# Down projection: accumulators first written by ScalarE, the residual added in later blocks, stores in SP's queue

## The chip, the cores and the metric

The kernel runs on one core of one Trainium2 chip. A core has a matrix engine (TensorE, PE in the profile, with PEld for its weight loads), VectorE (DVE), ScalarE (ACT), GpSimd (POOL) and SyncE (SP), which run their own instruction streams and meet through semaphores. Matmuls write to PSUM, a small memory of banks of 128 x 512 fp32; DVE and ACT read it, POOL does not here. DMA transfers are issued by SP, ACT or POOL, each from its own in-order queue, and run beside the engines. The metric is the device time of one execution in microseconds; the median of three runs is compared.

## The reference

One inference step of one hybrid encoder layer, for a prompt of 1024 frames and a running stream of 64 frames, together 1088 rows of width 1024:

```python
h = _rms_norm(x, norm1_g)
parts = jnp.split(h @ w_in, np.cumsum(IN_SIZES)[:-1].tolist(), axis=-1)
...
x = x + jnp.concatenate([o_a, o_b, o_c], axis=-1) @ w_out
h = _rms_norm(x, norm2_g)
x = x + (jax.nn.silu(h @ w_gate) * (h @ w_up)) @ w_down
```

The three mixers between the two projections (a gated delta rule, a gated MLP over chunks, a sliding-window attention) do not matter here. What matters is the first norm of `x`, at the very start, and the last line: its hidden layer has 2816 columns, `w_down` is 2816 x 1024, and `x` on the right is the residual.

## The kernel before

**Number format.** Every fp32 operand of a matmul is kept as two numbers, a rounded one (`h`, made by an ACT copy) and the remainder (`l`, a DVE subtraction); a product takes three matmuls, hh, hl and lh.

**The start.** `x_load` (L254) brings a tile of 128 rows of `x`; its third argument is the issuing queue, POOL by default. SP issues x tile 0, then three weight loads with x tile 2 and the constants behind them; x tile 1 goes through POOL's queue (L270). `x_stat` (L290) sums squares on ACT (L293) and forms the reciprocal root on POOL with `gpow` (L284: a multiply-add, L287, and a power, L288). L315 does this for tiles 0 and 1, L316 and L317 scale both tiles on DVE, and everything that follows is released after the second scaling (`issue_after(first.ins)`). Then PE transposes the tiles (L303), DVE applies the gain, ACT rounds, and the input projection's matmuls (L95) run against weights split by `Weights.split` (L133: ACT copy into `hw`, DVE subtraction into `lw`).

**The down projection** (L1652 to L1958) runs over six blocks of hidden columns, `KB`: five of two groups of 256, the last of one. In a block there are four pairs of prompt tiles (`PAIRS`), each with seven steps (`STEPS`, a Strassen-like scheme in which step results are added along the way inside a PSUM bank), and two sample steps for the 64 stream rows. A step of a prompt pair has 6 matmuls of 128 x 512 (3 in block 5), a sample step 8 (4 in block 5), all from L1803 and L95. Block 0 runs pair 0, the sample, then pairs 1 to 3; the others begin with the sample.

After every step its bank is added to an accumulator `yf[t]`, a 128 x 1024 tile in SBUF. `y_add` (L1778) does that on DVE, reading PSUM and `yf`, writing `yf`. The step after next in the same bank (banks Y and Z; X is used once) accumulates onto what is there, so PE waits for the addition. In the sample the lower 64 partitions of the bank are first copied by ACT, and DVE makes two additions. The accumulator starts as the residual: `y_load` (L1772) takes a place in SBUF and loads the tile from `yd` in SP's queue, two tiles before block 0 and seven in it, at the steps in `y_when` (L1931).

In block 5 the additions of steps 0, 1 and 2 go through an ACT copy and a POOL addition (L1816, L1817). Those of steps 3 to 6 are the last of their halves: DVE adds, and `y_out` (L1782) stores 128 x 512 from ACT's queue. The two stream halves are stored after the first step of pair 1 (`outs`).

**Loads.** The hidden operand of a step, `w<-hd`, is loaded by `a_load` (L1759) into one of 20 slots of the pool `WS`. `fetch` (L1866) issues one load a step while the dictionary `AL` holds fewer than nine entries (seven while hidden stores are left). A step takes its entry out of `AL` (L1798); a sample step reads its entry and leaves it there (L1831). The weights `w_down` are loaded (L1698), combined on POOL (`diff`, L1706), rounded on ACT (`rnd`) and split on DVE (`sub`) for the next block at the step numbers in `ORDER`, through `prep` (L1750). In block 0 the last hidden values are also still being split and stored from ACT's queue by `hidden_late` (L1553).

**Order.** From the last unit of the hidden layer on, `manual_schedule` keeps all engines, SP among them, in the program's order: for each step the matmuls, the step's addition with its store if it has one (`flush`), `fetch`, residual loads, hidden stores, sample stores, `prep` (L1933 to L1952).

Of the kernel before, what the change touches and what calls it, by code (L numbers as in the profile page):

```python
# [12 lines left out]
ALU = mybir.AluOpType  # L13
# [40 lines left out]
def hybrid_step(ctx, tc, x_prompt, x_sample, cache_k, cache_v, st_gdn, st_conv, norm1_g, w_in, conv_w, a_log,  # L54
# [3 lines left out]
    V, A, G, T, SP = nc.vector, nc.scalar, nc.gpsimd, nc.tensor, nc.sync  # L58
# [17 lines left out]
    def sb(p, shape, tag, dt=F32, bufs=None):  # L76
        return p.tile(shape, dt, tag=tag, name=tag, bufs=bufs)
# [7 lines left out]
    def acopy(out, in_, scale=1.0):  # L85
        return A.activation(out=out, in_=in_, func=AF.Copy, scale=scale)  # L86
# [4 lines left out]
    def tt(out, in0, in1, op):  # L91
        return V.tensor_tensor(out=out, in0=in0, in1=in1, op=op)  # L92
# [155 lines left out]
    def x_rows(s, t):  # L248
        t0, np_, ns = SEGS[s]
        return (x_prompt[0, t0 + 128 * t:t0 + 128 * t + 128, :], 128) if 128 * t < np_ else (x_sample[0], 64)  # L250

    xs_tiles = {}

    def x_load(s, t, q=G):  # L254
        src, r = x_rows(s, t)
        x = sb(xp, [128, DM], "xs", bufs=3)
        q.dma_start(out=x[:r], in_=src)
        xs_tiles[s, t] = x
# [7 lines left out]
    prm1 = sb(gp, [128, 390], "tr", bufs=9)  # L266
    A.dma_start(out=prm1[0:8, 0:128], in_=norm1_g[0].rearrange("(k p) -> k p", p=128))
    W.load()
    W.load()
    x_load(0, 1)  # L270
    W.load()
    x_load(0, 2, SP)
    SP.dma_start(out=cst[:, 192:], in_=cst_in[:, 192:])
# [16 lines left out]
    def x_stat(x, r):  # L290
        jk = sb(wp, [128, DM], "xt2", BF16, bufs=2)
        ss = sb(cp, [128, 1], "ss", bufs=4)
        A.activation(out=jk[:r], in_=x[:r], func=AF.Square, accum_out=ss[:r])  # L293
        gpow(ss[:r], ss[:r], 1.0 / DM, EPS, mhalf)
        return ss
# [16 lines left out]
            acopy(h, t[:, :, :r])  # L312
            tt(xl[:, 4 * j:4 * j + 4, c0:c0 + r], t[:, :, :r], h.bitcast(F32), ALU.subtract)

    rstd = [x_stat(xs_tiles[0, t], 128) for t in range(2)]  # L315
    for t in range(2):  # L316
        first = V.tensor_scalar(out=xs_tiles[0, t], in0=xs_tiles[0, t], scalar1=rstd[t], scalar2=None, op0=ALU.mult)  # L317
    pb = ax()
    T.transpose(pb[:, :8], prm1[0:8, 0:128], ident[0:8, 0:8])
    g1T = sb(cp, [128, 8], "g1T")  # L320
    V.tensor_copy(out=g1T, in_=pb[:, :8])
    ctx.enter_context(tc.issue_after(first.ins))
    W.run(1)
    prm = sb(gp, [128, 390], "tr", bufs=9)
    SP.dma_start(out=prm[0:8, 0:128], in_=norm2_g[0].rearrange("(k p) -> k p", p=128))
    SP.dma_start(out=prm[8:9, 0:128], in_=gdn_g)
# [888 lines left out]
    yd = tc.dram_tile([9 * 128, DM], F32, name="yd")  # L1215
# [201 lines left out]
    WS = Slots([128, 4, 128])  # L1417
# [236 lines left out]
    PAIRS = ((0, 0, 0, 2), (0, 1, 1, 3), (1, 0, 4, 6), (1, 1, 5, 7))  # L1654
    RIGHT = ("B11", "T1", "T2", "B21", "T3", "B22", "T4")
    LAST = {0: "R1", 4: "T13", 5: "R2", 6: "T24"}
    D, AL, yf = {}, {}, {}
# [20 lines left out]
    y_places, outs = [], []  # L1678

    def block(t):  # L1680
        return t.rearrange("p a b -> p (a b)")
# [87 lines left out]
        SP.dma_start(out=v[:, :2 * len(kps)].bitcast(F32),  # L1769
                     in_=hs[2 * kps[0]:2 * kps[-1] + 2].rearrange("f p t -> p f t"))  # L1770

    def y_load(t, places=y_places):  # L1772
        p, tag, bufs = places.pop(0)
        yf[t] = sb(p, [128, DM], tag, bufs=bufs)
        r = 64 if t == 8 else 128
        SP.dma_start(out=yf[t][:r], in_=yd[128 * t:128 * t + r, :])

    def y_add(t, h, ps):  # L1778
        c = slice(512 * h, 512 * h + 512)
        tt(yf[t][:, c], ps, yf[t][:, c], ALU.add)  # L1780

    def y_out(t, h):  # L1782
        c = slice(512 * h, 512 * h + 512)
        dst = y_p[0, 128 * t:128 * t + 128, c] if t < 8 else y_s[0, :, c]
        A.dma_start(out=dst, in_=yf[t][:dst.shape[0], c])


    STEPS = ((0, "Y", ((0, 0, 0),)), (1, "Z", ((1, 1, 0),)), (2, "Y", ((0, 1, 0),)), (3, "X", ((0, 0, 1),)),
# [2 lines left out]
    def pair_steps(b, p):  # L1791
        kps, banks = KB[b], {}

        def step(n, bank, adds):
            fresh = bank not in banks
            if fresh:
                banks[bank] = mmb() if bank == "X" else ax()
            ps, a = banks[bank], AL.pop((b, p, n))  # L1798
            m = 0
            for k, kp in enumerate(kps):  # L1800
                bh, bl = D[kp][RIGHT[n]]
                for l, r in ((a[:, 2 * k], bh), (a[:, 2 * k], bl), (a[:, 2 * k + 1], bh)):
                    T.matmul(ps, l, r, start=fresh and m == 0, stop=m == 3 * len(kps) - 1,  # L1803
                             skip_group_check=not fresh)
                    m += 1
                if p == 3 and n in LAST:
                    PT.give(D[kp][LAST[n], "h"], D[kp][LAST[n], "l"])
            WS.give(a)

            def add():  # L1810
                for i, j, done in adds:
                    t = PAIRS[p][2 + i]
                    if b + 1 == len(KB) and not done:
                        slot = WS.take()
                        c = slice(512 * j, 512 * j + 512)
                        acopy(block(slot), ps)  # L1816
                        G.tensor_tensor(out=yf[t][:, c], in0=block(slot), in1=yf[t][:, c], op=ALU.add)  # L1817
                        WS.give(slot)
                        continue
                    y_add(t, j, ps)  # L1820
                    if done and b + 1 == len(KB):
                        y_out(t, j)
            later.append(add)

        return [lambda x=x: step(*x) for x in STEPS]

    def sample_steps(b):
        kps = KB[b]

        def step(j):  # L1830
            ps, v = ax(), AL[b]  # L1831
            m, last = 0, 4 * len(kps) - 1
            for k, kp in enumerate(kps):
                for i in range(2):
                    for w in D[kp]["B%d%d" % (i + 1, j + 1)]:
                        mm(ps, v[:, 2 * k + i], w, m == 0, m == last)
                        m += 1
            if j:
                WS.give(v)

            def add():
                slot = WS.take()
                tmp = block(slot)[:64]
                c = slice(512 * j, 512 * j + 512)
                acopy(tmp, ps[64:128, :])
                tt(yf[8][:64, c], ps[0:64, :], yf[8][:64, c], ALU.add)
                tt(yf[8][:64, c], tmp, yf[8][:64, c], ALU.add)
                WS.give(slot)
                if b + 1 == len(KB):
                    outs.append(lambda: y_out(8, j))  # L1850
            later.append(add)

        return [lambda j=j: step(j) for j in range(2)]
# [32 lines left out]
    for u in range(22):  # L1886
        if u == 21:
            ctx.enter_context(tc.manual_schedule(engines=ENGINES))
        sa, sb_ = unit_steps(u, 0), unit_steps(u, 1)
        if u == 0:  # L1890
            sa = [lambda: None] * 3 + [begun[k] for k in (2, 4, 5, 6)]
        steps = sa + sb_ if u in (0, 21) else [s for p in zip(sa, sb_) for s in p]
        for i, s in enumerate(steps):
            s()
            flush()
            for q in hid[:1] if u < 21 else ():
                if next(q, 1):
                    hid.remove(q)
            if u == 0 and i < 7:
                next(xs1, None)  # L1900
            if i >= 7 or u not in (0, 21):
                n = i - 7 if u in (0, 21) else i // 2
                if u in (0, 21) or i % 2:
                    WS.give(*WA[u].pop(PRODUCTS[n][0]))
            if i == 7 - (u > 0) and u + 1 < 22:
                w_sums(u + 1)
            if i >= 7 and u + 1 < 22:
                for n in ([i - 8] if 7 < i else []) + ([6] if i == 13 else []) if u == 0 else [i - 7]:
                    w_split(u + 1, PRODUCTS[n][0])
            if u == 21:  # L1910
                left_over(i)
                prep(0, i)
                if i in (7, 8):
                    y_load(PAIRS[0][i - 5])
                if i > 7:
                    fetch()
            if u == 20 and i == 8:
                PT.add(xa, "x0", 15)
                PT.add(xb, "x1", 11)
                prep(0, i - 14)  # L1920
        WA.pop(u)
        if u + 2 < 22:
            w_loads(u + 2)
# [6 lines left out]
    del y_places[7:]  # L1930
    y_when = {(0, 1): 8, (0, 3): 1, (0, 5): 3, (1, 1): 4, (1, 3): 6, (2, 1): 5, (2, 3): 7}  # L1931
    start = 0
    for i, (b, p, n, f) in enumerate(work):  # L1933
        if i and b > work[i - 1][0]:
            start = i
            prep(b, 99, 99, 99)
        f()
        flush()
        fetch()
        if b == 0 and (p, n) in y_when:  # L1940
            y_load(y_when[p, n])
        for q in hid[:1 if i < 4 else 2]:
            if next(q, 1):
                hid.remove(q)
                if not hid:
                    _ev.close()
                    dq, _dq = pool("ffne2", "right")
                    PT.add(dq, "f", 8, 8)
        if p == 1:
            while outs:  # L1950
                outs.pop()()
        prep(b + 1, i - start)  # L1952
    _dq.close()
    _xb.close()
# [33 lines left out]
```

## Time and profile before

| | us |
|---|---|
| median of 3 runs (1349.97 to 1350.61) | 1350.33 |
| the profiled execution's own time | 1349.63 |
| its span, first to last instruction | 1347.9 |
| PE busy | 1311.6 |
| DVE busy | 936.8 |
| ACT busy | 635.4 |
| POOL busy | 175.3 |

The span is what the trace covers; the 1.7 us between it and the time lie outside the instructions. Busy time is the union of an engine's instructions. Matmuls are pipelined, so a row's duration of 0.39 us for a matmul is its whole passage, and the next begins some 0.23 us after it. In rows of the timeline the first number is the start in us from the span's start, the second the duration, x the count of merged instructions; the bracket is the idle time before the first of them and what released it. Rows with a q behind the engine's name (SPq, ACTq) are issues of DMA transfers.

### The profile page before, as it was taken

To read this page: it belongs to the slowest core of one execution; us is meant where nothing else is said; L and a number is where in the kernel's file an instruction comes from. 1 tells how busy PE (TensorE), PEld (TensorE's weight loads), DVE (VectorE), ACT (ScalarE), POOL (GpSimd) and SP (SyncE) were. 2 spreads that over 40 slices of the span, in tenths; PEclk is the share of its full clock that TensorE was granted. 3 is DMA by queue.
4 is the path that set the end of the run, shared out by engine and by line. 5 is a ranking of instruction groups with operands and counts; after the bars stand their busy time and mean duration, and the time that the engine had idled before them with its cause. 6 is when DMAs were issued, how large, how long until landed. Compare 5 with 4: busy or idle time off the path is not lost.

```text
span 1347.9 us, 26489 instructions
## 1 busy us (share of the span) xinstructions
PE 1311.6 (97%) x9922; PEld 1169.9 (87%) x9922; DVE 936.8 (70%) x2190; ACT 635.4 (47%) x1629; POOL 175.3 (13%) x250
## 2 busy tenths in 40 slices
PE   6999999999999999998999999999999988999997
PEld 6988888888878887788999999999999976777784
DVE  5887866756577675588866776667766687767764
ACT  7677455562555553546545554455544532222202
POOL 3101120100111110100000000000000333232104
PEclk9999999999999999999999999999999999999999
DMA  8975654434455573152533553345433499666645
GB/s 263 350 259 190 230 181 162 153 126 159 163 172 173 205 263 113 73 194 81 160 115 125 177 159 124 110 137 177 147 122 116 148 340 326 220 220 239 214 144 199
DMA packets 183075, 243.63 MB, mean 181 GB/s; under 512 B 14523, under 2 KB 133792, under 8 KB 182946
## 3 DMA queue, kind: packets, MB, share of 16 engines
q1 hardware_dynamic: 174754, 229.34, 51.6%
q10 hardware_dynamic: 6704, 8.36, 1.7%
q0 software_dynamic: 1488, 4.23, 1.0%
q8 instruction: 78, 1.28, 0.4%
q14 instruction: 51, 0.42, 0.1%
HBM read 160.92 MB, written 81.04 MB: 180 GB/s over the span
## 4 chain that ended last, share of the span: by engine, by line
PE 82%; DVE 6%; issue 6%; POOL 2%; DMA 2%; ACT 2%; POOLq 0%; ACTq 0%; DVEq 0%
PE ax L1490 29%; PE mm L95 25%; PE ax L95 11%; PE ax L1803 8%; PE mm L1490 5%; DVE x L92 2%; PE mm L1803 1%; DMA hd<-w 1%; PE ax L303 1%; PE ax L531 1%; DVE tr L89 1%; POOL x L1817 1%; PE ax L866 1%; POOL ssk L288 1%; DMA xs<-in_x_prompt_dram 0%
## 5 line engine op out<-in xcount | busy, mean ns | idle before, releaser
L1490 PE MATMUL ax<-x,w 128*128 128x256 f32 (+1 forms) x2552 | 358.6, 287 | 0.0
L1490 PEld LDWEIGHTS ax<-x,w 128*128 128x128 f32 x2552 | 334.2, 190 | 0.3 <-ACT x L86 0.2
L92 DVE TENSOR_TENSOR w<-w,w 128x512 fp32r<-128x512 f32 (+1 forms) x242 | 164.4, 687 | 88.4 <-PE ax L1490 52.7
L95 PE MATMUL mm<-xh,hw 128*128 128x384 f32 (+1 forms) x432 | 151.6, 351 | 0.0
L95 PE MATMUL mm<-xl,hw 128*128 128x384 f32 (+1 forms) x432 | 142.7, 330 | 0.0
L95 PE MATMUL mm<-xh,lw 128*128 128x384 f32 (+1 forms) x432 | 142.2, 329 | 0.0
L1803 PE MATMUL ax<-x,w 128*128 128x512 f32 x480 | 132.7, 401 | 7.8 <-DVE x L92 7.6
L92 DVE TENSOR_TENSOR x<-ax,x 128x512 f32<-128x512 f32 (+1 forms) x144 | 98.3, 687 | 58.6 <-PE ax L1803 48.3
L1803 PEld LDWEIGHTS ax<-x,w 128*128 128x128 f32 x480 | 91.7, 193 | 31.4 <-DVE x L92 11.4
L1490 PE MATMUL ax<-xr,w 128*128 128x288 f32 x616 | 116.1, 296 | 1.2 <-DVE s L92 1.2
L86 ACT ACTIVATE w<-w 128x512 fp32r<-128x512 f32 x154 | 94.9, 624 | 38.5 <-PE mm L1490 14.9
L1490 PEld LDWEIGHTS ax<-xr,w 128*128 128x128 f32 x616 | 94.9, 188 | 1.5 <-DVE s L92 1.5
L95 PEld LDWEIGHTS mm<-xh,hw 128*128 128x128 f32 x432 | 81.1, 188 | 9.6 <-issue 6.8
L86 ACT ACTIVATE s<-ax 128x256 f32<-128x256 f32 (+1 forms) x132 | 52.0, 394 | 75.7 <-PE ax L1490 75.2
L95 PEld LDWEIGHTS mm<-xl,hw 128*128 128x128 f32 x432 | 81.5, 189 | 0.8 <-issue 0.3
L95 PEld LDWEIGHTS mm<-xh,lw 128*128 128x128 f32 x432 | 81.0, 188 | 0.6
L1803 PE MATMUL ax<-f,w 128*128 128x512 f32 x220 | 72.5, 399 | 2.8 <-ACT w L86 1.5
L89 DVE SCALAR_TENSOR_TENSOR tr<-tr,cw 128x384 f32<-128x384 f32 (+1 forms) x108 | 64.1, 594 | 12.7 <-ACT tr L86 11.3
L1706 POOL TENSOR_TENSOR w<-x 128x512 f32<-128x512 f32 x6 | 8.8, 1463 | 488.4 <-PE ax L1490 442.2
L1490 PE MATMUL mm<-x,w 128*128 128x256 f32 (+1 forms) x528 | 70.5, 289 | 0.0
L1490 PEld LDWEIGHTS mm<-x,w 128*128 128x128 f32 x528 | 67.9, 190 | 0.2 <-issue 0.2
L95 PE MATMUL mm<-hw,xh 128*128 128x256 f32 (+1 forms) x216 | 62.6, 294 | 0.0
(360 smaller groups left out, 2489.9 us busy)
## 6 DMA issues: line engine op xcount, KB each, us to landing
hd<-e SPq DMA_DIRECT2D x140, 256.0 KB, 2.4
w<-hd SPq DMA_DIRECT2D x140, 256.0 KB, 4.3
lw<-wk SPq DMA_DIRECT2D x46, 512.0 KB, 4.5
hw<-wk SPq DMA_DIRECT2D x46, 512.0 KB, 3.7
wr<-in_w_in_dram SPq DMA_DIRECT2D x28, 512.0 KB, 5.9
wk<-hw SPq DMA_DIRECT2D x25, 512.0 KB, 3.8
wk<-lw SPq DMA_DIRECT2D x25, 512.0 KB, 3.9
w<-in_ffn_w_gate_dram SPq DMA_DIRECT2D x44, 256.0 KB, 3.3
```

The costliest lines, as they stand in the source:

```text
L86: return A.activation(out=out, in_=in_, func=AF.Copy, scale=scale)
L89: return V.scalar_tensor_tensor(out=out, in0=in0, scalar=s, in1=in1, op0=op0, op1=op1)
L92: return V.tensor_tensor(out=out, in0=in0, in1=in1, op=op)
L95: return T.matmul(out, lhsT, rhs, start=start, stop=stop)
L288: G.tensor_tensor(out=out, in0=out, in1=e[:r, :n], op=ALU.pow)
L303: T.transpose(b[k // 4][:, (k % 4) * r:(k % 4) * r + r], x[:r, k * 128:k * 128 + 128], ident[:r, :r])
L531: T.transpose(b[u // 4][:, (u % 4) * 128:(u % 4) * 128 + 128], src(u).rearrange("p h i -> p (h i)"), ident)
L866: T.transpose(PTp[0:r0 + cnt, j, kv, :], P[:, kv, 128 * j:128 * j + r0 + cnt], ident)
L1490: T.matmul(ps[:, :NB[c]], a[:, k, :], b[:, k, :], start=first and i == 0, stop=i == 11, skip_group_check=not first)
L1706: eng.tensor_tensor(out=block(t), in0=a, in1=b, op=ALU.subtract)
L1803: T.matmul(ps, l, r, start=fresh and m == 0, stop=m == 3 * len(kps) - 1, skip_group_check=not fresh)
L1817: G.tensor_tensor(out=yf[t][:, c], in0=block(slot), in1=yf[t][:, c], op=ALU.add)
```

## The change

- In block 0 the accumulators' first values (steps 0, 1, 2 and 6 of each pair) are written by an ACT copy from PSUM instead of a DVE addition onto the residual. In the sample steps of block 0 DVE makes one addition instead of two.
- `y_load` becomes `y_take`, which takes the place without a load. The residual comes in blocks 1 to 4 by a generator `residual`: 18 halves (nine tiles), each loaded from `yd` into a `WS` slot by SP, added on DVE four steps later, and two more steps until the next half. The generator is advanced once a step from block 1 on.
- `y_out` issues its stores from SP's queue instead of ACT's.
- At the start x tile 1 is loaded in SP's queue between the first and the second weight. Statistics and scaling of tile 1 come after the first weight's split; what follows is released by tile 0's scaling.

```diff
     W.load()
+    x_load(0, 1, SP)
     W.load()
-    x_load(0, 1)
     W.load()
...
-    rstd = [x_stat(xs_tiles[0, t], 128) for t in range(2)]
-    for t in range(2):
-        first = V.tensor_scalar(out=xs_tiles[0, t], in0=xs_tiles[0, t], scalar1=rstd[t], scalar2=None, op0=ALU.mult)
+    def x_first(t):
+        rstd = x_stat(xs_tiles[0, t], 128)
+        return V.tensor_scalar(out=xs_tiles[0, t], in0=xs_tiles[0, t], scalar1=rstd, scalar2=None, op0=ALU.mult)
+
+    first = x_first(0)
...
     ctx.enter_context(tc.issue_after(first.ins))
     W.run(1)
+    x_first(1)
...
-    def y_load(t, places=y_places):
+    def y_take(t, places=y_places):
         p, tag, bufs = places.pop(0)
         yf[t] = sb(p, [128, DM], tag, bufs=bufs)
-        r = 64 if t == 8 else 128
-        SP.dma_start(out=yf[t][:r], in_=yd[128 * t:128 * t + r, :])
+
+    def residual():
+        for t in range(9):
+            r = 64 if t == 8 else 128
+            for j in range(2):
+                c = slice(512 * j, 512 * j + 512)
+                slot = WS.take()
+                SP.dma_start(out=block(slot)[:r], in_=yd[128 * t:128 * t + r, c])
+                for _ in range(4):
+                    yield
+                tt(yf[t][:r, c], block(slot)[:r], yf[t][:r, c], ALU.add)
+                WS.give(slot)
+                yield
+                yield
...
     def y_out(t, h):
...
-        A.dma_start(out=dst, in_=yf[t][:dst.shape[0], c])
+        SP.dma_start(out=dst, in_=yf[t][:dst.shape[0], c])
...
+                    if b == 0 and (n < 3 or n == 6):
+                        acopy(yf[t][:, 512 * j:512 * j + 512], ps)
+                        continue
                     y_add(t, j, ps)
...
-                tt(yf[8][:64, c], ps[0:64, :], yf[8][:64, c], ALU.add)
-                tt(yf[8][:64, c], tmp, yf[8][:64, c], ALU.add)
+                if b:
+                    tt(yf[8][:64, c], ps[0:64, :], yf[8][:64, c], ALU.add)
+                    tt(yf[8][:64, c], tmp, yf[8][:64, c], ALU.add)
+                else:
+                    tt(yf[8][:64, c], ps[0:64, :], tmp, ALU.add)
...
         if p == 1:
             while outs:
                 outs.pop()()
+        if b:
+            next(rest, None)
         prep(b + 1, i - start)
```

More of the change, by code (lines that the diff above doesn't have):

```diff
@@ L1913, in hybrid_step @@
                 if i in (7, 8):
-                    y_load(PAIRS[0][i - 5])
+                    y_take(PAIRS[0][i - 5])
                 if i > 7:
@@ L1932, in hybrid_step @@
     start = 0
+    rest = residual()
     for i, (b, p, n, f) in enumerate(work):
@@ L1940, in hybrid_step @@
         if b == 0 and (p, n) in y_when:
-            y_load(y_when[p, n])
+            y_take(y_when[p, n])
         for q in hid[:1 if i < 4 else 2]:
```

## The prediction

> **What bounds the kernel now.** First the page, then the stretches (each row: stretch, length, busy time and instructions of PE, weight load, DVE, ACT, POOL, granted clock, DMA share, GB/s).
>
> ```profile
> span 1347.9 us, 26489 instructions
> PE 1311.6 (97%) x9922; PEld 1169.9 (87%) x9922; DVE 936.8 (70%) x2190; ACT 635.4 (47%) x1629; POOL 175.3 (13%) x250
> ```
>
> ```profile
> 1100.00:1110.00 10.00, 7.16 (x26) 5.48 (x25) 7.64 (x11) 2.68 (x6) 5.86 (x5) 0.80 1.02 359
> 1120.00:1130.00 10.00, 6.31 (x20) 4.75 (x21) 8.71 (x9) 1.91 (x3) 5.30 (x4) 0.83 0.97 336
> 1150.00:1170.00 20.00, 20.00 (x88) 16.11 (x87) 14.05 (x20) 2.54 (x4) 5.39 (x4) 1.00 0.58 178
> 1320.00:1330.00 10.00, 7.16 (x27) 4.71 (x27) 3.96 (x7) 1.68 (x3) 5.92 (x5) 1.00 0.85 280
> ```
>
> PE is busy 97% of the span, so time can be won only where it stands still. The change touches four places: the start, block 0 of the down projection (1088 to 1142 us: PE idle, clock below 1, DMA full), blocks 1 to 4 (PE full, DVE at 70%) and block 5 (from 1317 us: PE idle again). I go through them in order.
>
> **The start.** Timeline rows (start, duration, engine, line, operation, count, idle before and its releaser); the first and last rows are from the chain of waits.
>
> ```profile
> 1.33 6.48 DMA xs<-in_x_prompt_dram
> 5.95 0.18 POOL L287 TENSOR_SCALAR ss<-ss 128x1 f32<-128x1 f32 x1
> 9.34 1.40 POOL L288 TENSOR_TENSOR ss<-ss,mhalf 128x1 f32<-128x1 f32 x2
> 9.95 1.58 DVE L317 TENSOR_SCALAR xs<-xs,ss 128x1024 f32<-128x1024 f32 x2 [4.33 <-ACT hw L86]
> 14.22 0.39 PE L95 MATMUL mm<-hw,xh 128*128 128x264 f32 x1
> 23.19 8.66 PE mm L95 x70
> ```
>
> Tile 0's statistics are through L287 at 6.13, but its power (L288) runs at 9.34, behind tile 1's L287, which waits for tile 1's load through POOL's queue (landed at 7.81). So tile 0's scaling on DVE starts at 9.95. With tile 1 taken out of that order the power takes half of 1.40, and the scaling can start near 6.9: 3.0 us earlier. The load moves to SP's queue behind the first weight, and W1, W2 and x tile 2 stand behind it by one issue more. From 10 us on, DVE has weights and tiles to split without a pause, so not all 3.0 need reach 23.19, where PE runs through. Bounds: 0 and -4.0; I take -2.5, near the measured lag.
>
> **Block 0.** PE's rows in it; from the chain of waits the sample matmuls that begin blocks 1 and 2, with 36 undisturbed matmuls between; ACT's rows (the last is an eviction of block 5); the times to landing of the residual loads.
>
> ```profile
> 1087.84 4.26 PE L1803 MATMUL ax<-x,w 128*128 128x512 f32 x18
> ...
> 1106.83 2.93 PE L1803 MATMUL ax<-x,w 128*128 128x512 f32 x6 [2.84 <-DVE x L92]
> ...
> 1126.59 10.13 PE L1803 MATMUL ax<-x,w 128*128 128x512 f32 x36 [3.69 <-DVE x L92]
> ```
>
> ```profile
> 1142.19 3.74 PE ax L95 x16
> ...
> 1151.88 8.35 PE ax L1803 x36
> ...
> 1185.35 3.69 PE ax L95 x16
> ```
>
> ```profile
> 1107.69 0.42 ACT L86 ACTIVATE w<-ds 128x256 fp32r<-128x256 f32 x1 [5.32 <-POOL g L1570]
> ...
> 1116.87 1.06 ACT L86 ACTIVATE f<-xr 128x1024 fp32r<-128x1024 f32 x1 [4.83 <-DMA hd<-w]
> ...
> 1120.86 1.04 ACT L86 ACTIVATE xr<-xr 128x1024 fp32r<-128x1024 f32 x1
> ...
> 1319.30 0.60 ACT L86 ACTIVATE w<-ax 128x512 f32<-128x512 f32 x1 [0.37 <-PE ax L1803]
> ```
>
> ```profile
> DMA to landing us min/median/max: 2.6/3.6/9.0
> ```
>
> Block 0 takes 1142.2 - 1087.8 = 54.4 us, block 1 with the same matmuls 43.2: at most 11.2 us to win, namely the two waits (2.84 + 3.69) and their clock loss. The change moves 16 evictions (four in each of four pairs) from DVE to ACT, drops two sample additions, and takes nine loads of up to 512 KB out of a stretch whose DMA share is 1. But ACT is in order too, and here it issues the last hidden stores: it stands still 5.32 us to 1107.69 and 4.83 us to 1116.87, just where pair 1's evictions would queue. So pair 1's wait (2.84) stays in another form: the eviction would come at 1107.69 + 0.42 + 0.6 = 1108.7 at the latest, 1.9 us after PE went on before, and sooner as the loads leave the DMA queues. Pair 2's wait goes, for ACT's rounding there is done by 1121.9: 3.69, and the clock loss behind it, 36 matmuls in 10.13 instead of 8.35: 1.8. That gives -5.5, which I take; bounds +1.9 and -11.2. What is late next is ACT.
>
> **Blocks 1 to 4.** DVE's and POOL's rows in block 1.
>
> ```profile
> 1158.09 1.81 DVE L92 TENSOR_TENSOR x<-x,x 128x1024 fp32r<-128x1024 f32 x1
> ...
> 1168.63 0.69 DVE L92 TENSOR_TENSOR x<-ax,x 128x512 f32<-128x512 f32 x1 [0.70 <-PE ax L1803]
> ...
> 1176.25 1.22 DVE L92 TENSOR_TENSOR x<-x,x 128x1024 fp32r<-128x1024 f32 x1
> ```
>
> ```profile
> 1160.37 1.29 POOL L1706 TENSOR_TENSOR w<-x,w 128x512 f32<-128x512 f32 x1 [1.55 <-PE ax L1803]
> ```
>
> 18 additions of about 0.69 come in, one every six steps, at steps 4, 10, 16, 22 and 28 of a block. A step gives DVE 1.39 us, of which 0.69 is the accumulation and 0.70 idle, so an addition alone in its step costs nothing (4, 16; 28 is covered by the sample steps behind it). At 10 it follows a split of 1.81, slowed beside POOL, and meets POOL's next operation; at 22 it stands ahead of a split of 1.22. At 22 addition and split ask 0.69 + 1.22 of 0.70 idle, 1.2 too much; at 10 the split was already 1.1 over, and the addition fills the idle that made it good. The step after next adds to the same bank, 0.70 after the accumulation's normal end, so PE waits 0.4 to 0.5. Blocks 1 to 3 have both steps, block 4 step 10 only: 7 x 0.43 = 3.0 us. Bounds: 0, and 18 x 0.69 = 12.4 if loads came late each time (the load has four steps, 5.6 us, against a median of 3.6; SP runs ahead here). The 4.4 MB are covered by a DMA share of 0.58.
>
> **Block 5.** The key is the order of SP's queue. In before, SP holds only loads; the stores are on ACT.
>
> ```profile
> L1764 SPq DMA_DIRECT2D w<-hd x168: 319/320/1267, 1077.7 to 1331.2; - x168
> ```
>
> ```profile
> w<-hd SPq DMA_DIRECT2D x8, 128.0 KB, 2.1
> ```
>
> ```profile
> w<-hd SPq DMA_DIRECT2D x16, 128.0 KB, 3.8
> ```
>
> ```profile
> 1319.11 0.39 PE L1803 MATMUL mm<-x,w 128*128 128x512 f32 x1
> ...
> 1333.85 0.39 PE L1803 MATMUL mm<-x,w 128*128 128x512 f32 x1
> ...
> 1339.33 0.96 PE L1803 MATMUL ax<-f,w 128*128 128x512 f32 x3 [0.46 <-ACT w L86]
> ...
> 1340.13 0.39 PE L1803 MATMUL mm<-x,w 128*128 128x512 f32 x1
> ...
> 1342.79 0.96 PE L1803 MATMUL ax<-f,w 128*128 128x512 f32 x3 [0.17 <-DVE x L92]
> ```
>
> ```profile
> 1341.08 0.69 DVE L92 TENSOR_TENSOR x<-mm,x 128x512 f32<-128x512 f32 x1 [2.87 <-PE mm L1803]
> ...
> 1343.21 1.29 DVE L92 TENSOR_TENSOR x<-ax,x 128x512 f32<-128x512 f32 x2 [0.48 <-POOL x L1817]
> ```
>
> The last load starts at 1331.2. In the program it stands behind step 3 of pair 3 (the mm matmul at 1340.13), since `fetch` keeps nine entries and six of them are the sample keys never removed from `AL`: three steps of reach. SP reached it 9 us early because no load waits for DVE. Now four stores per pair stand between the loads, each waiting for its accumulation, and each load behind it must be used three steps later.
>
> The loop in a pair: step 3 starts at 0; its accumulation ends 1.64 later (1340.13 to 1341.77); the store issues, 0.4; the load for step 6 issues and lands after L; PE goes on 0.1 later. So step 6 starts 2.2 + L after step 3, where the trace has 1342.79 - 1340.13 = 2.66. The same again from step 6 (accumulation ends at 1343.21 + 1.29 = 1344.50, 1.71 after its start) to step 2 of the next pair, and 0.80 to its step 3 (1339.33 to 1340.13). From step 3 of pair 0 to step 6 of pair 3 are 7 such legs and 3 x 0.80: 7 x (2.2 + L) + 2.4, against 1342.79 - 1319.11 = 23.7 now. L is 2.1 in 1300 to 1315 us, where these loads run alone, and 3.8 in block 5, beside stores. Block 5 stretched spreads the same bytes over more time, but a store now stands ahead in the same queue; I take 2.8: 37.4, so +13.7 us. Bounds: +8.8 (L = 2.1) and +20.7 (L = 3.8). That ACT no longer issues stores is in this sum: the 0.46 that PE waits for ACT goes, but what is late next are loads.
>
> **The sum**, against the profiled execution's 1349.63 us (span 1347.9), 0.70 below the median 1350.33 to which I apply it: -2.5 - 5.5 + 3.0 + 13.7 = +8.7, 1359.0 us.
>
> **Rivals.** *The loads still run ahead.* If SP's loads are not held by the stores (another order of the queue, or slots filled earlier), block 5 gains instead: the pair's period of 1340.13 - 1333.85 = 6.28 falls towards its 21 matmuls, 4.9, plus 0.5 of evictions, 0.9 x 3.5 pairs = -3. Sum -2.5 - 5.5 + 3.0 - 3 = -8.0: 1342.3, faster. Against it: from the last unit of the hidden layer on all engines keep the program's order, and `y_out` stands ahead of `fetch`. The Trainium skill ("DMA: Bandwidth & Descriptors", Issuing engines are not separate DMA queues) says that DMAs of all issuers share the same 16 engines and that a second issuer saves only issue time; by that the move alone would cost nothing, which is this rival. The rows agree on the sharing, but show nothing of a wait ahead of an issue.
>
> *The gains cancel it.* Block 0 wins all of 11.2 and the start 4.0, the loads take 2.1: -15.2 + 3.0 + 8.8 = -3.4; with half of that excess gain about +1: 1351. It decides where block 5 costs under what start and block 0 give.
>
> *The clock falls too.* Two 3.4 us stretches of equal length, one that lost the clock and one that did not, and what followed the first:
>
> ```profile
> 1102.65:1106.06 3.41, 1.34 (x6) 0.76 (x5) 3.38 (x6) 0.00 (x0) 1.26 (x1) 1.00 1.03 366
> 1106.06:1112.89 6.83, 6.06 (x14) 4.80 (x15) 3.65 (x8) 1.67 (x4) 1.96 (x2) 0.50 1.04 380
> 1324.50:1327.90 3.40, 1.65 (x6) 1.05 (x6) 0.69 (x1) 1.13 (x3) 1.30 (x1) 1.00 1.05 379
> ```
>
> With PE idle 2.07 us of 3.41 the clock halved, with 1.75 idle it held. A leg of 5.0 us with 2.1 of matmuls leaves 2.9 idle, mostly in one piece. Each leg holds one step of three matmuls (0.7), and 0.8 more per pair: doubled, 7 x 0.7 + 3 x 0.8 = 7.3 at most: 1366. The Trainium skill ("TensorE: Matmul & The Clock Gate", What's actually happening) has the clock halve after an idle window of about 3.4 us; by that a gap of 2.9 alone would not do it, yet the first row above lost it with less.
>
> *Addition stalls.* 12.4 in place of 3.0: 1368, little likely, since SP runs ahead in blocks 1 to 4.
>
> **Chances.** Forecast 0.52 (1354 to 1363); clock or additions as well 0.20 (1363 to 1372); cancelled 0.12 (1348 to 1353); loads ahead, or everything gained, 0.16 (1340 to 1348). The range leaves out the faster rival's most and the top of the slowest: 1346 to 1370. Slower by over 0.2% (2.7 us, about what a measurement of this kernel can tell from no change) 0.73, within 0.12, faster 0.15. The likeliest case's own range is 1354 to 1363.
>
> **What would show it.** In block 5, SP's hidden loads start right behind stores and PE's idle is released by those loads, with 10 to 11 us between mm steps of pairs 2 and 3. In block 0, pair 2's wait of 3.69 is gone and PE waits for ACT in pair 1. In blocks 1 to 3, short waits of PE for DVE near steps 12 and 25. The first L95 matmul starts near 11. I am wrong if SP's last hidden load still starts 9 us ahead of its place, or if the start reorders so that 23.19 does not move.

## The result and the profile after

| | before | after |
|---|---|---|
| median | 1350.47 (4 runs, 1349.97 to 1352.37) | 1358.55 (4 runs, 1358.10 to 1361.63) |
| ratio, 95% interval | | 1.0062 (1.0044 to 1.0080) |
| profiled execution, its span | 1349.63, 1347.9 | 1358.69, 1356.8 |

The kernel became 8.1 us slower; 1359.0 was predicted. First the head of the page of after: PE's work is what it was, its busy time 4.8 us longer.

```profile
span 1356.8 us, 26525 instructions
...
PE 1316.4 (97%) x9922; PEld 1171.6 (86%) x9922; DVE 938.9 (69%) x2190; ACT 645.7 (48%) x1645; POOL 177.9 (13%) x249
```

Where the 8.9 us of the spans arose is read from the starts of blocks: the first matmul of block 0, then each block's first sample matmul. In the timeline of after these are, for blocks 0 and 1:

```profile
1088.08 4.30 PE L1818 MATMUL ax<-x,w 128*128 128x512 f32 x18
...
1133.66 0.40 PE L95 MATMUL ax<-x,w 128*128 128x512 f32 x1
```

The 1142.19 that the prediction shows for block 1 of before is from the chain of waits, which leaves out up to 0.2 us of what overlaps the engine before; that matmul's own start is 1142.03, and the table takes own starts. Lengths in us:

| stretch | before | after | difference | predicted |
|---|---|---|---|---|
| up to block 0 | 1087.84 | 1088.08 | +0.2 | -2.5 |
| block 0 | 54.18 | 45.58 | -8.6 | -5.5 |
| blocks 1 to 4 | 172.87 | 175.59 | +2.7 | +3.0 |
| block 5 | 32.95 | 47.50 | +14.5 | +13.7 |
| sum | | | +8.9 | +8.7 |

**Block 0 and the blocks behind it.** PE's rows with idle time in the timeline of after, two of block 0 and three of blocks 1 to 3:

```profile
1105.67 1.66 PE L1818 MATMUL ax<-x,w 128*128 128x512 f32 x6 [1.41 <-ACT x L86]
...
1122.55 5.78 PE L1818 MATMUL ax<-x,w 128*128 128x512 f32 x24 [1.47 <-DVE x L92]
```

```profile
1170.71 0.97 PE L1818 MATMUL ax<-f,w 128*128 128x512 f32 x3 [0.32 <-DVE x L92]
1214.58 0.98 PE L1818 MATMUL ax<-x,w 128*128 128x512 f32 x3 [0.33 <-DVE x L92]
1228.67 0.50 PE L1818 MATMUL ax<-f,w 128*128 128x512 f32 x1 [0.41 <-DVE x L92]
```

The wait of 2.84 in pair 1 is one of 1.41 for ACT, the 3.69 in pair 2 one of 1.47, still for DVE. The granted clock is 1 all through block 0. In the later blocks PE stops for DVE by 0.2 to 0.6 at a time, six times in all. Step by step, the starts of the matmuls show where the 2.7 arose: in each of blocks 1 to 3 after falls behind before by 0.35 to 0.45 us from step 12 to step 14 and by about 0.6 from step 24 to step 26. Block 4 shows neither.

**Block 5.** The page's group of PE, then two stretches of the chain of waits:

```profile
L1818 PE MATMUL ax<-f,w 128*128 128x512 f32 x220 | 76.0, 414 | 13.7 <-DMA w<-hd 10.9
```

```profile
1340.25 0.70 DVE x L92
1340.96 0.02 issue
1340.97 0.34 SPq L1800
1341.31 0.04 issue
1341.36 0.02 SPq L1767
1341.37 0.03 issue
1341.40 2.99 DMA w<-hd
1344.40 0.04 issue
1344.44 0.97 PE ax L1818 x3
```

Read downwards, this is the loop: addition, store, load, matmuls. SP issues the load only when the store ahead of it has been issued, and that waits for DVE. The load takes 2.99 and PE stands meanwhile. PE's rows at both ends of the seven legs:

```profile
1313.46 0.40 PE L1818 MATMUL mm<-x,w 128*128 128x512 f32 x1
...
1346.98 0.40 PE L1818 MATMUL mm<-x,w 128*128 128x512 f32 x1
...
1351.96 0.93 PE L1818 MATMUL ax<-f,w 128*128 128x512 f32 x3 [2.48 <-DMA w<-hd]
```

The last leg takes 1351.96 - 1346.98 = 4.98, predicted 5.0; all of them 38.5, predicted 37.4. The rest fits the clock (stretches of after: length, busy time and instructions of PE, weight load, DVE, ACT, POOL, granted clock, DMA share, GB/s):

```profile
1316.66:1320.07 3.41, 1.25 (x4) 0.78 (x5) 1.38 (x2) 0.00 (x0) 0.28 (x1) 1.00 0.83 259
...
1326.89:1330.31 3.42, 0.94 (x3) 0.48 (x3) 1.10 (x2) 0.00 (x0) 0.00 (x0) 1.00 0.84 243
...
1340.55:1343.97 3.42, 1.88 (x6) 0.97 (x6) 1.09 (x2) 0.00 (x0) 0.00 (x0) 1.00 0.74 240
```

```profile
1320.07:1323.48 3.41, 3.24 (x7) 1.67 (x6) 0.00 (x0) 1.20 (x2) 1.30 (x2) 0.50 0.78 233
1330.31:1340.55 10.24, 8.35 (x18) 5.58 (x18) 1.85 (x4) 1.79 (x3) 3.86 (x3) 0.50 0.43 134
```

Behind the stretches with 2.2 and 2.5 us of idle PE the clock is at half, behind the one with 1.5 it is not. The mm step of pair 2, in the half-clock stretch, came 12.2 us behind that of pair 1, where 10.5 and 10.9 are the other two distances.

### The profile page after: what moved, and what is told of

Read it like the earlier page. It is cut to its first block, busy times and chain, and to the rows that moved or that the text cites. A ratio compares the mean times of both kernels' runs of the same rounds, so it can differ in the third digit from the quotient of the medians.

```text
span 1356.8 us, 26525 instructions
## 1 busy us (share of the span) xinstructions
PE 1316.4 (97%) x9922; PEld 1171.6 (86%) x9922; DVE 938.9 (69%) x2190; ACT 645.7 (48%) x1645; POOL 177.9 (13%) x249
## 4 chain that ended last, share of the span: by engine, by line
PE 81%; DVE 8%; issue 5%; ACT 2%; POOL 2%; DMA 2%; SPq 0%; ACTq 0%; DVEq 0%; POOLq 0%
PE ax L1493 29%; PE mm L95 24%; PE ax L95 11%; PE ax L1818 8%; PE mm L1493 5%; DVE x L92 3%; PE mm L1818 1%; DMA w<-hd 1%; DVE tr L89 1%; PE ax L303 1%; PE ax L534 1%; DVE w L92 1%; PE ax L869 1%; POOL ssk L288 1%; DMA wr<-in_w_in_dram 0%
## 5 line engine op out<-in xcount | busy, mean ns | idle before, releaser
L95 PE MATMUL mm<-xh,hw 128*128 128x384 f32 (+1 forms) x432 | 151.6, 351 | 0.0
L95 PE MATMUL mm<-xl,hw 128*128 128x384 f32 (+1 forms) x432 | 142.6, 330 | 0.0
L95 PE MATMUL mm<-xh,lw 128*128 128x384 f32 (+1 forms) x432 | 142.3, 329 | 0.0
L92 DVE TENSOR_TENSOR x<-ax,x 128x512 f32<-128x512 f32 (+1 forms) x126 | 85.9, 687 | 53.3 <-PE ax L1818 47.1
L86 ACT ACTIVATE w<-w 128x512 fp32r<-128x512 f32 x154 | 94.9, 624 | 38.0 <-PE mm L1493 15.3
L95 PEld LDWEIGHTS mm<-xh,hw 128*128 128x128 f32 x432 | 81.1, 188 | 9.6 <-issue 6.8
L1818 PE MATMUL ax<-f,w 128*128 128x512 f32 x220 | 76.0, 414 | 13.7 <-DMA w<-hd 10.9
L95 PEld LDWEIGHTS mm<-xl,hw 128*128 128x128 f32 x432 | 81.5, 189 | 0.8 <-issue 0.3
L95 PEld LDWEIGHTS mm<-xh,lw 128*128 128x128 f32 x432 | 81.0, 188 | 0.6
L1818 PEld LDWEIGHTS ax<-f,w 128*128 128x128 f32 x220 | 41.9, 195 | 29.9 <-DVE x L92 8.2
```

Of the source, the lines that this page charges most:

```text
L95: return T.matmul(out, lhsT, rhs, start=start, stop=stop)
```

## The experiments

Each kernel was timed beside the kernel before on its chip. All of them in one table; stage lengths are from one profiled execution each, and where that lay well off the median the text says so.

| kernel | median, us | ratio to before, interval | block 0 | 1 to 4 | block 5 |
|---|---|---|---|---|---|
| after | 1358.55 | 1.0062 (1.0044 to 1.0080) | 45.6 | 175.6 | 47.5 |
| after, stores on ACT | 1345.40 | 0.9960 (0.9946 to 0.9974) | 45.5 | 175.7 | 33.4 |
| after, reach of nine | 1343.22 | 0.9942 (0.9926 to 0.9958) | 46.9 | 175.2 | 30.6 |
| before, stores on SP | 1365.70 | 1.0102 (1.0087 to 1.0118) | 53.0 | 173.1 | 46.9 |
| after, power of tile 0 first | 1360.88 | 1.0073 (1.0053 to 1.0094) | 46.1 | 175.7 | 47.3 |
| after, first writes by DVE | 1362.15 | 1.0090 (1.0075 to 1.0105) | 49.2 | 175.6 | 50.0 |
| after, loads put back | 1368.09 | 1.0121 (1.0105 to 1.0136) | 54.5 | 175.7 | 49.5 |
| after, loads put back beside | 1364.42 | 1.0101 (1.0086 to 1.0116) | 50.1 | 175.6 | 48.8 |
| after, no residual additions | 1355.97 | 1.0036 (1.0022 to 1.0050) | 45.6 | 172.5 | 46.8 |
| after, additions at free steps | 1357.18 | 1.0049 (1.0034 to 1.0064) | 49.6 | 172.9 | 48.3 |
| before, reach of nine | 1349.19 | 0.9990 (0.9981 to 0.9998) | 54.0 | 172.2 | 36.1 |
| both repairs, stores on SP | 1341.57 | 0.9933 (0.9920 to 0.9945) | 46.9 | 173.3 | 30.4 |
| both repairs, stores on ACT | 1344.79 | 0.9949 (0.9934 to 0.9964) | 49.6 | 173.3 | 32.9 |

### Is it the stores' queue? (three kernels)

The stores back on ACT:

```diff
-        SP.dma_start(out=dst, in_=yf[t][:dst.shape[0], c])
+        A.dma_start(out=dst, in_=yf[t][:dst.shape[0], c])
```

> The changed kernel with one part undone: the stores of the results are issued from ACT's queue again. Theory (stores wait in SP's in-order queue for their additions and hold the hidden loads behind them): the 14.5 us that block 5 lost come back; block 5 falls from 47.5 us to about 33, the time to about 1344, faster than both kernels. Rival (block 5 suffers from something else, for example from the clock or from the residual additions that end in block 4): block 5 stays near 47 and the time near 1358.

Block 5 fell to 33.4 us and the time to 1345.4. The kernel before with the opposite edit alone:

```diff
-        A.dma_start(out=dst, in_=yf[t][:dst.shape[0], c])
+        SP.dma_start(out=dst, in_=yf[t][:dst.shape[0], c])
```

> The kernel before with one part of the change alone: the stores of the results in SP's queue. Theory: block 5 grows by 13 to 15 us (33.0 to about 47), blocks 0 to 4 stay, time about 1364, ratio 1.010. Rival (the loss needs the other parts, for example a DVE that runs late after the residual additions): less than 5 us, time below 1356.

Block 5 grew by 13.9 us to 46.9 with none of the other parts there (the profiled execution was the fastest of four, 2.8 us under the median). Its page has the same row as after:

```profile
L1803 PE MATMUL ax<-f,w 128*128 128x512 f32 x220 | 74.9, 408 | 13.9 <-DMA w<-hd 13.7
```

So this one line of the change carries the whole loss, but that does not say why. A store in SP's queue could cost through its wait, or through its transfer and its issue. The third kernel leaves it there and lengthens the loads' reach:

```diff
-            ps, v = ax(), AL[b]
+            ps, v = ax(), AL.pop(b) if j else AL[b]
```

> The changed kernel with the stores left in SP's queue, but a sample step takes its key out of the dictionary, so that the limit of nine counts only loads that are still to be used: in block 5 a load is issued up to nine steps ahead in the program instead of three. Theory (a load is late only because its place in SP's queue is three steps ahead of its use and a store that waits stands in front): nearly all of the 14.5 us come back without moving a store; block 5 takes 33 to 36 us, time 1344 to 1347. Rival (stores and loads in one queue slow each other as transfers, or the issue time on SP counts): little comes back, block 5 above 43 us, time above 1354.

Block 5 takes 30.6 us, less than before the change. From its chain of waits the longest load, then from the timelines SP's last load and stores, and PE's waits for loads:

```profile
1328.25 0.03 SPq L1767
...
1328.38 4.95 DMA w<-hd
```

```profile
1330.84 0.46 SPq L1767 DMA_DIRECT2D w<-hd  x1
1331.39 6.55 SPq L1800 DMA_DIRECT2D out_dram<-x  x6
```

```profile
1331.33 0.50 PE L1818 MATMUL ax<-xr,w 128*128 128x512 f32 x1 [0.57 <-DMA w<-hd]
1333.37 0.50 PE L1818 MATMUL mm<-x,w 128*128 128x512 f32 x1 [0.26 <-DMA w<-hd]
```

Stores and loads alternate in the queue as in after, but six of the stores now follow the last load, and PE waits 0.8 us for loads in all of block 5, where in after it waits 11.6 (10.9 of them in the group above). The wait in front of the issue was the cost, not the transfer: a load that takes 4.95 us, longer than any of block 5 in after (3.6), hardly shows.

### Is it the same in the kernel before? (one kernel)

> The kernel before with one edit that is no part of the change: a sample step takes its key out of the dictionary, so the loads reach nine steps ahead. Theory (in the kernel before SP is never held, so its loads run early with a reach of three as well; only their number under way differs): block 5 gains at most the 2.3 us that the changed kernel with this edit had below it (33.0 to 30.6 us), blocks 0 to 4 stay; time 1347 to 1350.5. Rival (the gain in the run with the longer reach came from elsewhere): time unchanged at 1350.5, block 5 at 33.

The edit is the one line above. The time fell by 1.5 us (ratio 0.9981 to 0.9998), inside the theory's range. The stage went against it: block 5 took 36.1 us in the profiled execution, which at 1351.96 was the slowest of twelve. PE's longest waits in it are for ACT:

```profile
1325.32 0.97 PE L1803 MATMUL ax<-f,w 128*128 128x512 f32 x3 [1.67 <-ACT w L86]
1329.90 0.50 PE L1803 MATMUL ax<-xr,w 128*128 128x512 f32 x1 [2.93 <-ACT w L86]
```

In ACT's order the evictions of steps 0 to 2 stand behind stores. The version with both repairs, tried on either queue below, shows the same. Of the 15.3 us that the reach gave the changed kernel, the kernel before had about 1.5 to gain (0.3 to 2.6 by the interval): there the loads were not held.

### The start (one kernel)

On POOL tile 1's statistics are put behind tile 0's power:

```diff
-        G.tensor_tensor(out=out, in0=out, in1=e[:r, :n], op=ALU.pow)
+        return G.tensor_tensor(out=out, in0=out, in1=e[:r, :n], op=ALU.pow)
...
-        gpow(ss[:r], ss[:r], 1.0 / DM, EPS, mhalf)
+        pows.append(gpow(ss[:r], ss[:r], 1.0 / DM, EPS, mhalf))
...
-    x_first(1)
+    with tc.issue_after(pows[0].ins):
+        x_first(1)
```

> The changed kernel with one more order: on POOL the statistics of x tile 1 are issued after the power of tile 0. Theory (tile 0's power waits only for the multiply-add of tile 1 ahead of it on POOL): the power runs near 6.3 us, DVE's scaling of tile 0 starts near 7.0 instead of 9.99, and PE runs through 2 to 3 us earlier than at 23.1 us; time about 1356. Rival (the weights, not the statistics, set the start): the scaling starts at 7 but the matmuls of the input projection begin near 14 and run through near 23 as before; time within 0.5 us of 1358.6.

POOL and DVE in the timelines, after first, this kernel second:

```profile
6.01 0.19 POOL L287 TENSOR_SCALAR ss<-ss 128x1 f32<-128x1 f32 x1
9.13 0.19 POOL L287 TENSOR_SCALAR ss<-ss 128x1 f32<-128x1 f32 x1 [2.93 <-ACT xt L293]
9.40 1.38 POOL L288 TENSOR_TENSOR ss<-ss,mhalf 128x1 f32<-128x1 f32 x2
...
9.99 0.75 DVE L317 TENSOR_SCALAR xs<-xs,ss 128x1024 f32<-128x1024 f32 x1 [4.45 <-POOL ss L288]
```

```profile
6.30 0.56 POOL L288 TENSOR_TENSOR ss<-ss,mhalf 128x1 f32<-128x1 f32 x1
...
6.89 0.75 DVE L319 TENSOR_SCALAR xs<-xs,ss 128x1024 f32<-128x1024 f32 x1 [1.15 <-POOL ss L288]
```

The change did not do here what it says: both powers still stand behind both multiply-adds, since the order it asks for binds DVE, the scaling's engine, and not POOL. Once POOL has the order, the scaling is 3.1 us earlier, as worked out; the first matmul of the input projection starts at 12.87 instead of 14.46, and PE runs through from 22.60 instead of 23.09. So of 3.1 us, 0.5 arrived, nearer the rival's "as before" than the theory's 2 to 3. Half of it was lost ahead of the first matmul, for ACT rounds `xh` only at 12.20, behind six copies of weights. A further 1.1 was lost on PE (stretches of after, then of this kernel; the PE column counts matmuls):

```profile
14.50:16.00 1.50, 1.50 (x8) 1.46 (x7) 1.50 (x4) 1.19 (x3) 0.56 (x1) 1.00 1.13 285
16.00:17.50 1.50, 1.50 (x14) 1.50 (x13) 1.50 (x4) 0.32 (x3) 0.97 (x2) 1.00 0.71 192
```

```profile
14.50:16.00 1.50, 1.50 (x9) 1.50 (x9) 1.50 (x4) 0.32 (x3) 0.96 (x2) 1.00 1.05 353
16.00:17.50 1.50, 1.50 (x8) 1.50 (x8) 0.97 (x2) 1.50 (x2) 0.00 (x0) 1.00 1.00 339
17.50:18.50 1.00, 1.00 (x10) 1.00 (x10) 0.69 (x1) 0.22 (x2) 0.00 (x0) 1.00 0.33 58
```

PE is full in all five, but runs at half pace until 16.0 in after and until 17.5 here: it began earlier and became fast later. Whether the 0.5 lasts cannot be read: block 0 begins at 1089.1 instead of 1088.1, but in the kernels of this document whose start is that of after it begins anywhere from 1088.0 to 1089.6. The time does not tell it from after.

### What relieves block 0? (three kernels)

The first writes by DVE, without the residual loads:

```diff
-                        acopy(yf[t][:, 512 * j:512 * j + 512], ps)
+                        V.tensor_copy(out=yf[t][:, 512 * j:512 * j + 512], in_=ps)
```

> The changed kernel, but the accumulators' first values in block 0 are written by a DVE copy from PSUM, not by ACT; the residual stays out of block 0. Theory of the prediction (block 0 is relieved because 16 evictions leave DVE): block 0 goes back from 45.6 us to above 51, PE's waits for DVE return at pairs 1 and 2; time above 1363. Rival (it is relieved because the residual loads left a stretch in which the DMA engines are full, so that what DVE splits arrives earlier): block 0 stays below 48, time within 2 us of 1358.6.

The loads of the residual put back at their old steps, into the same places:

```diff
         yf[t] = sb(p, [128, DM], tag, bufs=bufs)
+        r = 64 if t == 8 else 128
+        SP.dma_start(out=yf[t][:r], in_=yd[128 * t:128 * t + r, :])
```

> The changed kernel with the residual loads of block 0 put back beside it: each place is loaded from the residual when it is taken, as before, and then overwritten by ACT's first write; the residual is added in the later blocks all the same, so the loads are traffic alone. Theory (evictions on ACT are what relieves block 0): block 0 stays at 45 to 48 us, time below 1361. Rival (the loads are the burden): block 0 above 50 us, time above 1363. If ACT's first writes wait for these loads, their idle time says so, and that part counts for neither.

And the same loads into slots that nothing reads, each pair of slots held until the next:

```diff
+        while spare:
+            WS.give(spare.pop(0))
+        r = 64 if t == 8 else 128
+        for j in range(2):
+            spare.append(WS.take())
+            SP.dma_start(out=block(spare[-1])[:r], in_=yd[128 * t:128 * t + r, 512 * j:512 * j + 512])
```

> The changed kernel with the same loads of the residual put back into block 0, this time into slots that nothing reads, so that no ACT write waits for them: traffic alone, and two slots held. Theory (the DMA engines are full in block 0, and these 4.4 MB hold back what DVE and ACT wait for there): block 0 goes from 45.6 us to above 51, time above 1363, with PE's waits released by ACT or DVE as in the kernel before. Rival (what cost in the run with loads into the accumulators' places was the wait of the ACT writes for those loads): block 0 below 48, time below 1361.

With the loads back and ACT still writing, block 0 took 54.5 us, as long as before the change. The view of DMA transfers in 1088 to 1134 us (KB each, median us to landing), after first:

```profile
w<-hd SPq DMA_DIRECT2D x29, 256.0 KB, 5.4
hd<-w ACTq DMA_DIRECT2D x14, 256.0 KB, 4.3
```

```profile
w<-hd SPq DMA_DIRECT2D x25, 256.0 KB, 5.7
hd<-w ACTq DMA_DIRECT2D x14, 256.0 KB, 7.1
```

```profile
1106.83 2.93 PE L1820 MATMUL ax<-x,w 128*128 128x512 f32 x6 [2.59 <-ACT x L86]
1113.13 10.07 PE L1820 MATMUL ax<-x,w 128*128 128x512 f32 x36 [1.96 <-ACT x L86]
...
1129.90 7.37 PE L1820 MATMUL ax<-x,w 128*128 128x512 f32 x24 [2.57 <-DVE x L92]
```

The hidden stores land after 7.1 us instead of 4.3. (That 25 loads are issued instead of 29 says nothing: there are 25 too in the kernel whose first writes are by DVE, without these loads.) PE's long waits are back, two of three for ACT now. Part of the 54.5 is ACT's waiting for these loads, so the kernel with the loads beside counts: the traffic (and two slots fewer) costs 4.5 us in block 0 and 5.9 by the medians, its interval clear of after's. It keeps a longer wait in pair 1:

```profile
1109.02 2.93 PE L1826 MATMUL ax<-x,w 128*128 128x512 f32 x6 [4.74 <-ACT x L86]
```

That falls just short of the "above 51" expected, and refutes the rival's "below 48".

DVE in ACT's place gave 49.2 in the profile and 3.6 us by the medians, between both expectations, and the intervals overlap those of after. The profiled execution was the slowest of its four. Nor does one profile fix the length of block 0: the additions at free steps (below) leave it alone, and yet it took 49.6 us there in the slowest of six executions, with pair 2's wait at 2.58 and a granted clock of 0.60 in the 3.4 us behind it:

```profile
1126.32 7.38 PE L1816 MATMUL ax<-x,w 128*128 128x512 f32 x24 [2.58 <-DVE x L92]
```

The two versions with both repairs, alike in block 0, have 46.9 and 49.6. So the traffic's part rests on the times: all four of the kernel with the loads beside lie above all four of after, though the kernel with the power of tile 0 first, alike in block 0, reached 1364.6 once. Its size in block 0 is not fixed by one profile, and how the traffic delays PE is shown only in part: in that kernel the hidden stores land after 5.1 us, against 4.3 in after but 4.9 with the additions at free steps. The engine's part lies between nothing and 3.6 us and stays open.

### The additions of the residual (two kernels)

The 18 additions left out, the loads kept:

```diff
-                tt(yf[t][:r, c], block(slot)[:r], yf[t][:r, c], ALU.add)
```

> The changed kernel without the 18 additions of the residual; their loads stay. The output lacks the residual. Theory (the additions stop PE at steps 10 and 22, 0.43 us each time): blocks 1 to 4 fall from 175.6 us to 172.9, which is what they took in the kernel before; time about 1356. Rival (loads or the ACT writes of block 0 cost there): blocks 1 to 4 stay above 174.5.

Blocks 1 to 4 fell to 172.5 us. The loads cost nothing there; the additions cost 3.1. Then all 18 additions, at other steps:

```diff
                 WS.give(slot)
-                yield
-                yield
...
-        if b:
+        if b and i - start not in (9, 10, 12, 14, 17, 19, 22, 25, 28):
             next(rest, None)
```

> The changed kernel with the residual's generator advanced only at steps where DVE has no split near it (not at steps 9, 10, 12, 14, 17, 19, 22, 25 and 28), a load every four of those; the same 18 loads and additions. Theory (an addition alone in its step costs nothing): blocks 1 to 4 fall from 175.6 us to 173 to 173.8, time 1356 to 1357. Rival (each addition costs DVE time wherever it stands): they stay at 175 or more, time 1358.6 or later.

Blocks 1 to 4 fell to 172.9 us, with the additions. In four blocks two waits of PE are left, where the kernel before has two as well, of 0.42 and 0.39:

```profile
1204.62 0.96 PE L1816 MATMUL ax<-x,w 128*128 128x512 f32 x3 [0.42 <-DVE x L92]
...
1275.82 0.50 PE L1816 MATMUL ax<-x,w 128*128 128x512 f32 x1 [0.70 <-DVE x L92]
```

An addition alone in its step is all but free: the cost was its neighbours, as argued. The gain of 1.4 by the medians lies within the spread between runs; the stage lengths show it.

### Both repairs (two kernels)

The line for the reach and the lines for the additions' steps, as above; in the second kernel also the stores on ACT.

> The changed kernel with both repairs: loads that reach nine steps ahead in the program, and the residual's additions only at steps without a split beside them; stores in SP's queue. Theory (the repairs touch different blocks and add up): the 15.3 us of the longer reach and 1.4 to 2.7 of the additions, so 1340.5 to 1342, blocks 1 to 4 at 173 to 174 and block 5 at 30 to 31; faster than both kernels. Rival (loads further ahead hold slots that the additions' loads and DVE's combinations need): blocks 1 to 4 stay at 175, time 1343 or more.

> The same as the version with both repairs, but with the stores in ACT's queue. Theory (once the loads are issued early enough, the queue that issues a store no longer matters, except for ACT's issue time beside its evictions): within 2 us of that version, block 5 at 30 to 33 us. Rival (a store is better off in a queue that does not hold any load): 2 us faster or more, block 5 below 29.

Together they give 1341.57 us on SP, 0.7% under the kernel before, and block 5 falls to 30.4. Blocks 1 to 4 are at 173.3: the reach of nine and the additions do not disturb each other. With the stores on ACT it is 3.2 us more by the medians, over the 2 expected, though the intervals overlap; in the profiles block 5 is 2.5 longer, and there PE waits 3.3 us for ACT, on SP not at all. So in block 5 SP is the better queue once the loads are early enough: with ACT issuing, its evictions stand behind stores. Such a case in the first experiment (after, stores on ACT), ACT's rows of the timeline:

```profile
1320.95 1.21 ACTq L1800 DMA_DIRECT2D out_dram<-x  x2
1322.20 1.09 ACT L86 ACTIVATE w<-ax 128x512 f32<-128x512 f32 x2 [2.85 <-DMA w<-hd]
```

ACT computed nothing for 2.85 us, two stores' issue among them, and PE, which needed that eviction, stood 2.29 before it went on at 1323.34. The bracket names a load, but the eviction starts 0.04 us after the second store's issue ends (1322.16), and three more times in this block an eviction starts 0.10 to 0.11 us after the last of a run of stores. In the versions with stores on SP and a reach of nine no wait of PE for ACT is left.

## Why the prediction came out right, point by point

- **Block 5, +13.7: right in mechanism and size.** 14.5 was measured. A leg of 5.0 us was measured as 4.98, and the load in it, taken as 2.8, as 2.5 to 3.6 in the chain. What the rival on the clock foresaw came in part: two stretches at half clock, and about 1 us above the forecast.
- **The rival that loads still run ahead** was wrong for the change as made, but its price was right: with the reach lengthened, block 5 took 30.6 us, 2.3 below before, where -3 had been worked out. It also holds the answer to the cited rule (the Trainium skill, "DMA: Bandwidth & Descriptors", Issuing engines are not separate DMA queues): that a second issuer saves only issue time fits the transfers here, but 13.9 us hung on the issuer, because an issue waits in its engine's order.
- **Block 0, -5.5: a gain, forecast too small for this profile, and its price put on the part that is not shown.** The step that failed is "Pair 2's wait goes, for ACT's rounding there is done by 1121.9". It fell from 3.69 to 1.47 and was still DVE's. The prediction counted the nine loads among what the change takes out but priced only the evictions; the traffic of the loads is worth 4.5 us in one profile and 5.9 by the medians, the evictions nothing to 3.6. As predicted, pair 1's wait passed to ACT, and PE went on at 1105.67, where 1108.7 had been given as the latest. In this profile the clock no longer fell; in another of the same block 0 it did, so 8.6 is near the most that a profile shows.
- **Blocks 1 to 4, +3.0:** 2.7 measured, and the cause confirmed by removing the additions and by moving them away from the splits. Six of the seven losses that were forecast came at the steps that were named; the one of block 4 did not.
- **The start, -2.5: wrong.** The step that failed is "With tile 1 taken out of that order": the edit does not take it out, for POOL still runs both multiply-adds before both powers. The first L95 matmul, expected near 11, started at 14.46, and the 23.19 moved by only 0.1, to 23.09; that it would not move is one of the prediction's own signs of being wrong. And had the edit taken it out, 0.5 us would have reached that point instead of 2.5, since in the one profile of that kernel ACT rounds only at 12.20 and the earlier matmuls run at half pace for longer. This error of +2.7 and that of block 0, -3.1, cancelled by luck; the total was closer than its parts.
- **A slip in a sum.** In the rival of cancelling gains, half of the excess gain comes to +0.2 us, 1350.5, not to about +1; it stays within the range that was given its chance.

## What to carry to other kernels

- Before a DMA is moved to another engine's queue, list what stands behind it there and how far ahead of use each of those issues lies: a store that waits for compute turns every load behind it into one that is as late as the store. The cure is a longer reach in the program, not only another queue.
- A transfer that has nothing to do with the critical work can still cost where the DMA share is 1: moving 4.4 MB of residual out of such a stretch was worth 4.5 to 5.9 us here as far as one profile and the medians fix it, more than moving evictions to another engine was shown to be.
- Work added to an engine that has idle time is free or not by the step it lands in; look for the steps without a neighbour before adding up durations.

## What was not expected of the hardware

- At the start, full PE ran eight to nine matmuls in 1.5 us up to 16.0 (in the kernel with the power first up to 17.5), and in after 14 in the 1.5 us behind it, while the column of the granted clock reads 1.00 in all these rows: that column does not show the first slow stretch. The Trainium skill ("TensorE: Matmul & The Clock Gate", What's actually happening) has the clock rise after a busy window of about 3.4 us on a free-running grid. The rows agree as far as they go: PE became fast 5.2 us after its unbroken work began in after (10.80), and 6.7 us after in the other kernel (10.82).
- The clock halved again after stretches in which PE was busy 1.25 and 0.94 of 3.41 us, and held after one with 1.88, so no wholly idle stretch of that length was needed in this kernel. Where the Trainium skill asks for an idle window (the same page and section), the rows decide.
